# Storing the first eight finished row tiles one place earlier in the transfer order of a streamed matmul with scale and addend

## The chip, the cores and the metric

The kernel runs on one core of a Trainium2 chip. The metric is the device time of one execution in microseconds; a lower one is better. Three runs of the kernel before the change took 209.27, 209.72 and 210.06 us, a median of 209.72 us. A further execution was recorded by the profiler.

## The reference

```
batch, m, k, n = 16, 512, 1024, 768
x      : (16, 512, 1024) float32
weight : (1024, 768)     float32
add    : (16, 512, 768)  float32
out = scale * matmul(x, weight) + add_value      # scale = 0.1
```

With the batch flattened, 8192 rows of 1024 numbers are multiplied by a 1024 x 768 weight; the product is scaled and an addend of the same shape as the result is added.

## The kernel before

**Tiling.** The 8192 rows are 64 row tiles of 128 rows, numbered 0 to 63 (T, line 53). In three blocks (BLOCKS, line 9) a partition of the on-chip memory holds consecutive rows of the operand, so that a transfer of eight row tiles is one run of 32 KB for each partition for x, and of 24 KB for addends and results. In the text "rows 32 to 39" means row tiles 32 to 39 of x, "addends" those of add_value, "results" those of the output.

**Memory.** `xs` is a ring of 16 row tiles of x (X_SLOTS, line 10). `ao` is a ring of 32 row tiles (A_SLOTS, line 11), in which an addend is overwritten by its result: addends 32 to 39 go to the place of results 0 to 7 and can be loaded only after these are stored. `va` has two buffers of four row tiles in bfloat16, `xt` four transposed row tiles, `mm` four products in PSUM.

**Engines.** There is no scheduler: each engine has its own program, written out by hand, and all meet in semaphores.

- SyncE (`sync_engine`, line 120) issues every transfer in the order of the string STREAM (line 22), in which `x32+8` means rows 32 to 39, `a` addends, `w` the weight and `o` results. Ahead of each transfer it waits for whatever that transfer needs: for x, that ScalarE and GpSimd have moved away the rows whose slots are overwritten (lines 128 and 129); for addends from 32 on, that the results of the same slots have landed in memory (line 135); for results, that VectorE has made them (line 137). An engine's waits are in order, so everything behind a waiting transfer waits as well. All 28 transfers go to one hardware queue. Each transfer signals its landing on one of eight semaphores in turn ("lanes", line 83), and before a lane is used again SyncE waits for the earlier transfer on it (line 125).
- ScalarE and GpSimd (`mover`, line 140) cast x to bfloat16 and regroup it, each one half of a move of four row tiles (MOVE, line 20): move 8 takes rows 32 to 35, move 9 rows 36 to 39. A move waits for the landing of its rows (line 146) and for the `va` buffer (line 148), which comes free when the pairs of two moves ago have been transposed.
- VectorE (`vector_engine`, line 160) casts the weight, transposes two row tiles at a time (`turn`, line 169) and joins product and addend (`finish`, line 182). Pair p is row tiles 2p and 2p + 1; pair 16 holds rows 32 and 33. The order is finish(p), then turn(p + 2).
- TensorE (`tensor_engine`, line 219) multiplies pair after pair; pair p needs turn(p) and, for its place in PSUM, finish(p - 2).

The last transfer, results 60 to 63, is issued behind all of these (line 243).

Of the kernel before, what the change touches and what calls it, by code (L numbers as in the profile page):

```python
# [19 lines left out]
MOVE = 4  # L20

STREAM = """
    x0+4 w0+8 x4+8 a0+8 a8+8 x12+4 x16+8 a16+8 x24+8 a24+8 x32+8 o0+8 o8+8 a32+8 x40+8
    a40+8 x48+8 x56+4 o16+8 o24+8 a48+4 x60+4 a52+4 a56+8 o32+16 o48+4 o52+8 o60+4
"""

# [252 lines left out]
```

## Time and profile before

| | us |
|---|---|
| median of the three runs | 209.72 |
| lowest and highest run | 209.27 and 210.06 |
| profiled execution, its own time | 209.87 |
| its span in the profile | 208.1 |
| busy in that span: TensorE matmul | 167.7 (81%) |
| busy: VectorE | 122.9 (59%) |
| busy: ScalarE | 139.3 (67%) |
| busy: GpSimd | 139.9 (67%) |

The span runs from the first to the last thing that the profiler saw; 209.87 less 208.1 lies outside it. PE is TensorE, DVE VectorE, ACT ScalarE, POOL GpSimd; SPq is the queue of instructions of SyncE, which issues the transfers. Digits in strips are tenths of a slice, 40 slices to a span. The table of transfers gives for each group the number of issues, the kilobytes of one, and the median time from the issue to the landing, waiting in the queue included. A timeline row gives the start, the length, engine, line and operation, what is written and read, the number of instructions and, in brackets, the idle time ahead of the first and what ended it.

### The profile page before, as it was taken

What the parts mean: (1) busy time and instruction counts of PE and PEld (TensorE: products, weight loads), DVE (VectorE), ACT (ScalarE), POOL (GpSimd) and SP (SyncE); (2) the same over time, 40 slices, a digit from 0 to 9 for tenths busy, and PEclk for the clock granted to TensorE, in tenths of its full rate; (3) what the DMA queues carried; (4) which work ended last, traced back from release to release, by engine and by line L of the source; (5) the groups of instructions that cost most, each with busy time, mean ns of one, the idle gap of its engine ahead of it and who ended that gap; (6) DMA issues with size and microseconds to landing.
All of it is one profiled execution on the core that took longest, in us unless ns stands there. A gap on an engine that the chain in (4) does not pass through costs nothing.

```text
span 208.1 us, 2174 instructions
## 1 busy us (share of the span) xinstructions
PE 167.7 (81%) x1008; PEld 50.4 (24%) x512; DVE 122.9 (59%) x66; ACT 139.3 (67%) x153; POOL 139.9 (67%) x156
## 2 busy tenths in 40 slices
PE   0001994969999999999999999994999999999500
PEld 0000231313333333333333333321333333333100
DVE  0037309646777777777777777738677759776300
ACT  2495199989799896969694069999998969000000
POOL 0399399999799997969694059999999979000000
PEclk9999999999999999999999999999999999999975
DMA  6999999999999999999999999999999999998993
GB/s 249 452 408 447 409 453 444 409 457 403 436 461 409 425 463 416 367 411 439 439 427 438 419 441 450 403 428 447 435 409 432 427 439 449 449 453 364 454 411 161
DMA packets 4035, 87.06 MB, mean 418 GB/s; under 512 B 448, under 2 KB 448, under 8 KB 448
## 3 DMA queue, kind: packets, MB, share of 16 engines
q1 hardware_dynamic: 4032, 87.03, 97.9%
q14 instruction: 3, 0.02, 0.0%
HBM read 61.87 MB, written 25.17 MB: 418 GB/s over the span
## 4 chain that ended last, share of the span: by engine, by line
DMA 43%; PE 25%; POOL 21%; issue 3%; DVE 2%; SPq 1%; POOLq 0%; DVEq 0%
DMA xs<-in_x_dram 31%; POOL va L157 21%; PE mm L232 16%; DMA out_dram<-ao 12%; PE mm L207 9%; DVE xt L177 1%; DVE ao L188 1%; SPq L115 0%; SPq L113 0%; SPq L117 0%; POOLq L150 0%; SPq L106 0%; DVEq L106 0%; SPq L274 0%; SPq L237 0%
## 5 line engine op out<-in xcount | busy, mean ns | idle before, releaser
L232 PE MATMUL mm<-w_bf,xt 128*128 128x512 bf16 x496 | 163.8, 382 | 26.9 <-DVE w_bf L167 19.8
L157 POOL CAST va<-xs 32x1024 bf16<-32x1024 f32 (+1 forms) x152 | 139.7, 919 | 36.8 <-DMA xs<-in_x_dram 22.4
L157 ACT CAST va<-xs 32x1024 bf16<-32x1024 f32 (+1 forms) x152 | 138.0, 908 | 36.6 <-DMA xs<-in_x_dram 23.4
L207 PE MATMUL mm<-w_bf,xt 128*128 128x256 bf16 x512 | 140.2, 274 | 0.8
L232 PEld LDWEIGHTS mm<-w_bf,xt 128*128 128x128 bf16 x512 | 50.4, 98 | 144.6 <-issue 138.7
L177 DVE STREAM_TRANSPOSE xt<-va 128x1024 f32<-128x1024 f32 x32 | 65.2, 2038 | 32.0 <-POOL va L157 30.6
L188 DVE SCALAR_TENSOR_TENSOR ao<-mm,ao 128x1536 f32<-128x1536 f32 x32 | 56.0, 1754 | 42.5 <-PE mm L207 39.4
L167 DVE CAST w_bf<-ao 128x3072 bf16<-128x3072 f32 x2 | 3.8, 1948 | 0.0
L143 ACT ACT_TABLE_LOAD x1 | 1.3, 1283 | 0.9 <-SPq L237 0.9
L260 POOL MEMSET const-float32-0.0<- 128x1 f32 x1 | 0.1, 98 | 0.2 <-issue 0.2
L260 POOL MEMSET const-bfloat16-1.0<- 128x1 bf16 x1 | 0.1, 101 | 0.0
L260 POOL MEMSET const-float32-1.0<- 128x1 f32 x1 | 0.1, 98 | 0.0
L260 POOL MEMSET const-uint8-127<- 128x1 uint8 x1 | 0.1, 98 | 0.0
## 6 DMA issues: line engine op xcount, KB each, us to landing
xs<-in_x_dram SPq DMA_DIRECT2D x6, 4096.0 KB, 20.8
ao<-in_add_value_dram SPq DMA_DIRECT2D x7, 3072.0 KB, 25.2
out_dram<-ao SPq DMA_DIRECT2D x5, 3072.0 KB, 24.8
xs<-in_x_dram SPq DMA_DIRECT2D x4, 2048.0 KB, 13.3
out_dram<-ao SPq DMA_DIRECT2D x1, 6144.0 KB, 33.9
ao<-in_weight_dram SPq DMA_DIRECT2D x1, 3072.0 KB, 14.1
ao<-in_add_value_dram SPq DMA_DIRECT2D x2, 1536.0 KB, 14.6
out_dram<-ao SPq DMA_DIRECT2D x2, 1536.0 KB, 19.8
```

The costliest lines, as they stand in the source:

```text
L143: eng.preload_act_table(mybir.ActivationFunctionType.Copy)
L157: copy(va[q % VA_BUFS][32 * b:32 * b + 32, t:t + step, a, :], src[32 * a:32 * a + 32, t:t + step, b, :]).then_inc(count, step // 2)
L167: eng.tensor_copy(w_bf[:, h:h + 4, :], ao[:, W_SLOT + h:W_SLOT + h + 4, :]).then_inc(casts, 4)
L177: eng.transpose(xt[:, 2 * half:2 * half + 2, :, :].rearrange("p i c (a m) -> p i c a m", a=4), pairs.rearrange("p i a (k c) -> p i c a k", ...
L188: eng.scalar_tensor_tensor(a, mm[:, q:q + 2, 0:N], float(scale), a, op0=mybir.AluOpType.mult, op1=mybir.AluOpType.add).then_inc(made, 2)
L207: return eng.add_instruction(mybir.InstMatmult(name=nc.get_next_instruction_name(), engine=eng.engine, ins=[eng.lower_ap(weights), eng.low ...
L232: eng.matmul(mm[:, q, 0:CUT], piece, w_bf[:, j, 0:CUT], **flags)
L260: nc = _bacc.Bacc("TRN2", target_bir_lowering=False, num_devices=1)
```

## The change

One word of the transfer order changes its place. Results 0 to 7 (`o0+8`) are issued ahead of rows 32 to 39 (`x32+8`) instead of behind them; results 8 to 15 follow behind these rows. Number and sizes of the transfers, slots, waits of each kind and the programs of the other engines stay. Since lanes are dealt out in the order of the list, results 0 to 7 and rows 32 to 39 exchange theirs (lanes 2 and 3), and the waits on them follow.

```diff
 STREAM = """
-    x0+4 w0+8 x4+8 a0+8 a8+8 x12+4 x16+8 a16+8 x24+8 a24+8 x32+8 o0+8 o8+8 a32+8 x40+8
+    x0+4 w0+8 x4+8 a0+8 a8+8 x12+4 x16+8 a16+8 x24+8 a24+8 o0+8 x32+8 o8+8 a32+8 x40+8
     a40+8 x48+8 x56+4 o16+8 o24+8 a48+4 x60+4 a52+4 a56+8 o32+16 o48+4 o52+8 o60+4
 """
```

## The prediction

> **What bounds the kernel now.** I read the page first: the busy strip of the transfers and the table of queues.
>
> ```profile
> span 208.1 us, 2174 instructions
> ...
> DMA  6999999999999999999999999999999999998993
> ...
> q1 hardware_dynamic: 4032, 87.03, 97.9%
> ```
>
> The 16 transfer engines are busy for 97.9% of the span, in nine tenths or more of nearly every slice, all from one queue. PE, the next busiest, has 81%. So the bound to test is the stream of 87.03 MB: an order of transfers can save time only where this stream pauses or slows, and lose time only where it makes it pause. The second view is the timeline of SyncE around the change, which says when each transfer was issued.
>
> ```profile
> 53.63 0.33 SPq L115 DMA_DIRECT2D xs<-in_x_dram  x1
> 54.00 0.43 SPq L117 DMA_DIRECT2D ao<-in_add_value_dram  x1
> 72.09 0.33 SPq L115 DMA_DIRECT2D xs<-in_x_dram  x1
> 72.52 0.85 SPq L118 DMA_DIRECT2D out_dram<-ao  x2
> 97.37 0.34 SPq L117 DMA_DIRECT2D ao<-in_add_value_dram  x1
> 97.81 0.70 SPq L115 DMA_DIRECT2D xs<-in_x_dram  x1
> 104.65 0.33 SPq L117 DMA_DIRECT2D ao<-in_add_value_dram  x1
> 111.81 0.33 SPq L115 DMA_DIRECT2D xs<-in_x_dram  x1
> ```
>
> In the order of the list these are rows 24 to 31, addends 24 to 31, rows 32 to 39, results 0 to 7 and 8 to 15 (one row; the two issues are 0.47 us apart), addends 32 to 39, rows 40 to 47, addends 40 to 47, rows 48 to 55. The table of transfers, asked for one issue at a time, gives the time to landing of the first seven and the ninth, in this order:
>
> ```profile
> xs<-in_x_dram SPq DMA_DIRECT2D x1, 4096.0 KB, 18.3
> ao<-in_add_value_dram SPq DMA_DIRECT2D x1, 3072.0 KB, 25.2
> xs<-in_x_dram SPq DMA_DIRECT2D x1, 4096.0 KB, 17.9
> out_dram<-ao SPq DMA_DIRECT2D x1, 3072.0 KB, 24.8
> out_dram<-ao SPq DMA_DIRECT2D x1, 3072.0 KB, 31.6
> ao<-in_add_value_dram SPq DMA_DIRECT2D x1, 3072.0 KB, 14.5
> xs<-in_x_dram SPq DMA_DIRECT2D x1, 4096.0 KB, 23.8
> ...
> xs<-in_x_dram SPq DMA_DIRECT2D x1, 4096.0 KB, 26.8
> ```
>
> Issue plus time to landing gives 71.9, 79.2, 90.0, 97.3, 104.6, 111.9, 121.6 and, for rows 48 to 55, 138.6 us. The differences are the time of one transfer at the head of the queue: 7.3 us for addends 24 to 31, 10.8 for rows 32 to 39, 7.3 each for the two stores and addends 32 to 39, 9.7 for rows 40 to 47. They follow one another in the order of issue with no hole, and a store costs what an addend load of its size does. Each was in the queue before its turn: rows 32 to 39 by 79.2 - 72.1 = 7.1 us, addends 32 to 39 by 104.6 - 97.4 = 7.2 us. The stream does not run dry here.
>
> It does not at its end either; the last two issues are:
>
> ```profile
> 187.00 0.33 SPq L118 DMA_DIRECT2D out_dram<-ao  x1
> ...
> 197.66 0.33 SPq L118 DMA_DIRECT2D out_dram<-ao  x1
> ...
> out_dram<-ao SPq DMA_DIRECT2D x1, 3072.0 KB, 16.6
> ...
> out_dram<-ao SPq DMA_DIRECT2D x1, 1536.0 KB, 9.5
> ```
>
> Results 52 to 59 land at 203.6; the last store was issued 5.9 us before that and lands at 207.2. So all that the engines make is ready with some 6 us to spare.
>
> **The change, step by step.** First: can results 0 to 7 be issued at their new place, right behind addends 24 to 31 (issue 54.00 + 0.43)? Their lane was last used by rows 4 to 11, long landed; they need finish(3).
>
> ```profile
> 46.76 1.70 DVE L188 SCALAR_TENSOR_TENSOR ao<-mm,ao 128x1536 f32<-128x1536 f32 x1
> ...
> 67.96 1.76 DVE L188 SCALAR_TENSOR_TENSOR ao<-mm,ao 128x1536 f32<-128x1536 f32 x1 [1.47 <-PE mm L207]
> ```
>
> That ended at 48.5, so the store goes out at about 54.5 without a wait, and nothing behind it on SyncE is held up. Rows 32 to 39 then wait for moves 0 to 5 as before and go out at 72.1; results 8 to 15 follow at 72.5 (finish(7) ended at 69.7). The store's issue moves from 72.5 to 54.5, where SyncE only waited for GpSimd: 0 us on any path.
>
> Second: the queue. Addends 24 to 31 land at 79.2 as before. Then results 0 to 7 take 7.3 us, to 86.5; rows 32 to 39 take 9.7 (as rows 40 to 47) to 10.8 us (as here), to 96.2 or 97.3; results 8 to 15 to 103.5 or 104.6. Behind those the order and the bytes are the same. I take 97.3 and 104.6, since nothing says that the slow stretch of 10.8 goes away. Rows 32 to 39 are thus 7.3 us later, results 0 to 7 are 10.8 us earlier, and the sum over the three is unchanged: 0 us.
>
> Third: what is fed earlier. Addends 32 to 39 wait for the landing of results 0 to 7 and can go out at 86.6 instead of 97.4. Their turn in the queue comes at 104.6 both times, so their lead grows from 7.2 to 18 us, and nothing is gained, because the lead was not used up before. Rows 40 to 47 stood behind them on SyncE; they go out at 91.0, when move 7 is done (82.24 + 8.69 in the rows below), for a turn at 111.9. Also 0 us.
>
> Fourth: what is fed later. Moves 8 and 9 need rows 32 to 39.
>
> ```profile
> 82.24 8.69 POOL L157 CAST va<-xs 32x1024 bf16<-32x1024 f32 x8 [1.42 <-DVE xt L177]
> 92.63 8.69 POOL L157 CAST va<-xs 32x1024 bf16<-32x1024 f32 x8 [1.70 <-DVE xt L177]
> 103.03 8.70 POOL L157 CAST va<-xs 32x1024 bf16<-32x1024 f32 x8 [1.71 <-DVE xt L177]
> 121.75 3.27 POOL L157 CAST va<-xs 32x512 bf16<-32x512 f32 x5 [10.03 <-DMA xs<-in_x_dram]
> ```
>
> Before, move 8 began at 92.63, held by VectorE and not by the rows, which had been there for 2.6 us. After rows land GpSimd begins 0.2 us later (121.75 against 121.6). So move 8 now begins at 97.5, 4.9 us later, and ends at 106.2; move 9 ends at 114.9 instead of 111.7. Who waits for them:
>
> ```profile
> 104.36 1.76 DVE L188 SCALAR_TENSOR_TENSOR ao<-mm,ao 128x1536 f32<-128x1536 f32 x1 [1.50 <-PE mm L207]
> 106.04 2.04 DVE L177 STREAM_TRANSPOSE xt<-va 128x1024 f32<-128x1024 f32 x1
> 109.56 1.76 DVE L188 SCALAR_TENSOR_TENSOR ao<-mm,ao 128x1536 f32<-128x1536 f32 x1 [1.49 <-PE mm L207]
> ...
> 116.47 2.00 DVE L177 STREAM_TRANSPOSE xt<-va 128x1024 f32<-128x1024 f32 x1
> ```
>
> turn(16) at 106.04 needs move 8. It would begin at 106.3 at the latest, 0.3 us late, and end at 108.4; TensorE takes pair 16 up only when pair 15 is done, at 109.5 by the wait of finish(15). That leaves 1.1 us. turn(18) at 116.47 needs move 9, done at 114.9: 1.6 us left. Rows 48 to 55 wait on SyncE for move 9, so their issue goes from 111.8 to 115.0; their turn in the queue is 138.6 - 9.7 = 128.9. And from 121.75 the movers start afresh from rows 40 to 47, which land when they did: GpSimd's 10.03 us of waiting there shrink by 3.2, and the lateness ends.
>
> A rule of the Trainium skill speaks against this fourth step. The row is the landing of addends 32 to 39 behind a store, 7.3 us after it. The page DMA: Bandwidth & Descriptors, section "Queues, rings and completion order", says that a transfer's landing signal is written only after every earlier write of the same transfer engine, and its section on one DMA's anatomy gives about 2 us of fixed cost, mostly the receipt of the write, heaviest for HBM. By these, rows 32 to 39, now behind a store, could be reported up to 2 us later; as an estimate turn(16) would end at 110.4 and TensorE would wait 0.9 us. By the row there is no such delay, and the sum stays at 0.
>
> So the sum on the profiled execution is 209.87 + 0 = 209.87 us; it stands 0.15 above the median of the runs, and the prediction in terms of that median is 209.7.
>
> The zero of step four has a cover, with a price if it goes: TensorE loses what rows 32 to 39 come later than 97.3 + 1.1 = 98.4. Behind that lies another cover, TensorE's only wait in the second half:
>
> ```profile
> 143.33 0.39 PE L232 MATMUL mm<-w_bf,xt 128*128 128x512 bf16 x1 [2.68 <-DVE xt L177]
> ```
>
> It waits for rows from 40 on, not for those of the change, so up to 2.7 us of lateness vanish in it; the 5.9 us at the last store are the third.
>
> **Rivals.** *The hand-over from loads to stores costs.* The three stretches of the queue around the first store, in the view of engine time by windows:
>
> ```profile
> 79.30:90.00 10.70, 10.65 (x66) 3.21 (x33) 7.72 (x5) 8.86 (x10) 8.80 (x10) 1.00 0.95 379
> 90.00:97.30 7.30, 7.25 (x46) 2.25 (x23) 5.78 (x4) 5.29 (x6) 5.37 (x6) 1.00 1.01 434
> 97.30:104.60 7.30, 7.30 (x47) 2.15 (x22) 4.33 (x4) 5.34 (x6) 5.35 (x6) 1.00 1.02 438
> ...
> 86.00:88.00 2.00, 1.95 (x13) 0.59 (x6) 1.27 (x1) 1.95 (x3) 1.88 (x3) 1.00 0.94 279
> ```
>
> The last column is GB/s. Rows 32 to 39, the load just ahead of the first store, ran at 379 and took 10.8 - 9.7 = 1.1 us more than rows 40 to 47. If that is the price of turning from loads to stores, the change adds one such turn, at 79.2 behind addends 24 to 31: 209.7 + 1.1 = 210.8, slower, deciding if all 16 engines pay it at every turn. Against it: the dip to 279 lies at 86 to 88, before the load is through at 90.0, and the next such turn pays less:
>
> ```profile
> 132.46 0.33 SPq L115 DMA_DIRECT2D xs<-in_x_dram  x1
> ...
> xs<-in_x_dram SPq DMA_DIRECT2D x1, 2048.0 KB, 11.2
> ```
>
> Rows 56 to 59 land at 143.7, 5.1 us behind rows 48 to 55, where half of 9.7 is 4.85: 0.2 us. The turn costs between 0 and 1.1 us; I take 0, as the dip precedes the store, and keep 1.1 for the range.
>
> *The late rows stop the stream.* Rows 32 to 39 reach TensorE late, products and stores follow late. It decides only if they land after 98.4 + 2.7 + 5.9 = 107.0; at 108.5 it would give 209.7 + 1.5 = 211.2. For it speaks that they have lost their lead over move 8; against it, 107.0 is later than the end of results 8 to 15, which stand behind them.
>
> *The slow microsecond goes with the old order.* If the 1.1 us come from rows 32 to 39 standing just there, they may be lost in the new one: 209.7 - 1.1 = 208.6, faster. For it: it is the only dip of this size in the rows above. Against it: every turn from load to store remains, and a dip tied to a moment stays.
>
> *The change does not do what it says.* The store is issued early but the engines serve rows 32 to 39 beside it rather than behind it. Then the rows land between 90.0 and 97.3, and with the same bytes the time is again 209.7. Against it, landings follow the order of issue in every row above.
>
> **How the numbers follow.** The forecast, no change and 209.7, gets 0.72; the hand-over 0.11, the late rows 0.02, the lost dip 0.11, the rival without effect 0.04. Half a per cent, 1.05 us, is what a measurement of this kernel can tell from no change: three runs already spread over 0.8 us. A hand-over at its lower price of 0.2 us stays within it; I give that 0.03 of the 0.11. So faster is 0.11, slower 0.08 + 0.02 = 0.10, and the same 0.72 + 0.04 + 0.03 = 0.79. The one unknown cost, the dip, sets the range: 208.6 where it goes, 210.8 where it comes twice; outside are the late rows.
>
> **What would show it.** Right: results 0 to 7 issued at about 54.5 and landed at about 86.5; rows 32 to 39 landed at 96.2 to 97.3; addends 32 to 39 issued near 86.6, rows 40 to 47 near 91.0, and the latter landed near 121.6 as before; move 8 on GpSimd released by the rows and not by VectorE; TensorE without a new wait at 109.5; the queue busy for about 98%. Wrong: a landing of rows 40 to 47 that differs from 121.6 by more than 1 us, a hole in the strip of the transfers behind 79 us, TensorE waiting at pair 16, or a last store issued after results 52 to 59 have landed.

## The result, and the profile after

| | before | after |
|---|---|---|
| median of 21 runs each, us | 209.31 | 210.03 |
| lowest and highest | 209.09 and 210.06 | 209.19 and 210.49 |
| profiled execution, own time and span | 209.87 and 208.1 | 210.11 and 208.3 |

The ratio of the two times is 1.0026, with a 95% interval of 1.0017 to 1.0034: slower by 0.54 us (0.36 to 0.71), less than half a per cent, but outside what chance explains. It is not the quotient of the two medians, which differ by 0.72 us; here and below the argument goes by the ratio and its interval. The profiled execution of before is a further one and slower than all but one of the 21, so the two traces differ by only 0.2 us in span; the difference of the kernels is to be looked for in where the traces lose time, not in their ends.

The page of the kernel after, first line and table of queues:

```profile
span 208.3 us, 2174 instructions
...
q1 hardware_dynamic: 4032, 87.03, 97.9%
```

The queue is as full as before. The timeline of SyncE, start and length in us:

```profile
53.68 0.33 SPq L115 DMA_DIRECT2D xs<-in_x_dram  x1
54.05 0.43 SPq L117 DMA_DIRECT2D ao<-in_add_value_dram  x1
54.59 0.38 SPq L118 DMA_DIRECT2D out_dram<-ao  x1
72.14 0.33 SPq L115 DMA_DIRECT2D xs<-in_x_dram  x1
72.56 0.38 SPq L118 DMA_DIRECT2D out_dram<-ao  x1
87.81 0.33 SPq L117 DMA_DIRECT2D ao<-in_add_value_dram  x1
91.09 0.33 SPq L115 DMA_DIRECT2D xs<-in_x_dram  x1
```

These are rows 24 to 31, addends 24 to 31, results 0 to 7, rows 32 to 39, results 8 to 15, addends 32 to 39 and rows 40 to 47. The table of transfers, asked for one issue at a time, gives their time to landing in the same order:

```profile
xs<-in_x_dram SPq DMA_DIRECT2D x1, 4096.0 KB, 18.4
ao<-in_add_value_dram SPq DMA_DIRECT2D x1, 3072.0 KB, 26.3
out_dram<-ao SPq DMA_DIRECT2D x1, 3072.0 KB, 33.2
xs<-in_x_dram SPq DMA_DIRECT2D x1, 4096.0 KB, 26.0
out_dram<-ao SPq DMA_DIRECT2D x1, 3072.0 KB, 32.9
ao<-in_add_value_dram SPq DMA_DIRECT2D x1, 3072.0 KB, 24.9
xs<-in_x_dram SPq DMA_DIRECT2D x1, 4096.0 KB, 31.3
```

Issue plus time gives the landings 72.1, 80.4, 87.8, 98.1, 105.4, 112.7 and 122.4. Two loads took longer than their size asks for: addends 24 to 31 took 8.3 us instead of 7.3, rows 32 to 39 took 10.4 instead of 9.7. Each is the load just ahead of a store. Before the change there was one such load here, rows 32 to 39 with 10.8 us. The slow microsecond has moved with the first store, from 86 to 88 us to 77 to 79, and a second, smaller one has appeared at the second. The window of the kernel after, to be held against the 279 GB/s of 86 to 88 us before:

```profile
77.00:79.00 2.00, 2.00 (x14) 0.59 (x6) 0.57 (x1) 1.95 (x3) 1.88 (x3) 1.00 1.03 344
```

The signals of landing show whom it hits. A transfer is worked off by 16 engines, and each adds its signal when its share has landed (each trace holds 448 such signals for 28 transfers). The time from the first signal to the last, here called the lag, is how far the last engine is behind the first (worked out from the semaphore events of the two traces, us):

```
landing of            before   after
rows 24 to 31          1.04     1.12
addends 24 to 31       1.05     1.81   <- a store follows, after
results 0 to 7         1.62     1.63
rows 32 to 39          1.59     2.47   <- a store follows, both
results 8 to 15        1.28     2.25
rows 48 to 55          1.62     2.49
rows 56 to 59          1.79     2.47   <- a store follows, both
addends 56 to 63       2.25     2.50   <- a store follows, both
results 60 to 63       2.29     2.39
first signal of it   204.91   205.01
```

The first engine is done at 204.9 to 205.0 both times; the span ends when the last one is. The packets of the change's second turn from loads to stores show it at work: from 95.29 us the engines in front send their first packets of the store, and of the 17 packets of rows 32 to 39 that start between 93.96 and 95.37 twelve take the usual 1.21 us, while five take 1.37 to 1.97. At the first store of the run all 16 engines are slowed: the 16 packets of addends 24 to 31 that start between 76.93 and 77.39 take 1.06 to 2.07 us instead of 0.92.

GpSimd and VectorE around move 8 and pair 16, in the timeline of the kernel after:

```profile
98.33 17.45 POOL L157 CAST va<-xs 32x1024 bf16<-32x1024 f32 x16 [7.33 <-DMA xs<-in_x_dram]
...
104.43 1.76 DVE L188 SCALAR_TENSOR_TENSOR ao<-mm,ao 128x1536 f32<-128x1536 f32 x1 [1.49 <-PE mm L207]
107.16 2.08 DVE L177 STREAM_TRANSPOSE xt<-va 128x1024 f32<-128x1024 f32 x1 [0.97 <-POOL va L157]
109.63 1.76 DVE L188 SCALAR_TENSOR_TENSOR ao<-mm,ao 128x1536 f32<-128x1536 f32 x1 [0.40 <-PE mm L207]
```

Move 8 waits for the rows and turn(16) for move 8, but finish(15) comes at 109.63 instead of 109.56. The late rows did not stop TensorE there: it shows no wait between 100 and 120 us.

### The profile page after: what moved, and what is told of

The parts are those of the page before. It is cut to its first block, busy times and chain, and to the rows that moved or that the text cites. A ratio compares the mean times of both kernels' runs of the same rounds, so it can differ in the third digit from the quotient of the medians.

```text
span 208.3 us, 2174 instructions
## 1 busy us (share of the span) xinstructions
PE 170.3 (82%) x1008; PEld 50.7 (24%) x512; DVE 122.8 (59%) x66; ACT 139.3 (67%) x153; POOL 139.9 (67%) x156
## 3 DMA queue, kind: packets, MB, share of 16 engines
q1 hardware_dynamic: 4032, 87.03, 97.9%
## 4 chain that ended last, share of the span: by engine, by line
PE 41%; DMA 26%; POOL 21%; DVE 5%; issue 2%; SPq 0%; DVEq 0%; POOLq 0%
PE mm L232 26%; DMA xs<-in_x_dram 26%; POOL va L157 21%; PE mm L207 14%; DVE xt L177 3%; DVE ao L188 2%; SPq L113 0%; SPq L115 0%; DVEq L106 0%; POOLq L150 0%; SPq L274 0%; SPq L106 0%; SPq L237 0%
## 5 line engine op out<-in xcount | busy, mean ns | idle before, releaser
L232 PE MATMUL mm<-w_bf,xt 128*128 128x512 bf16 x496 | 166.2, 385 | 26.8 <-DVE w_bf L167 19.9
```

The lines of the kernel that those rows point to most:

```text
L232: eng.matmul(mm[:, q, 0:CUT], piece, w_bf[:, j, 0:CUT], **flags)
```

## The experiments

Every time beside a ratio is the median of its runs, and the ratio stands against the kernel before, run on the same chip. Theory 1 is the hand-over: each place where the list turns from a load to a store costs in the transfers. Such a place is called a turn from here on; it has nothing to do with VectorE's `turn`. The list of before has three turns, that of the change four. Theory 2 is the late rows, which cost through TensorE.

**Both stores early.** Three turns, rows 32 to 39 later still.

```diff
-    ... a24+8 x32+8 o0+8 o8+8 a32+8 ...
+    ... a24+8 o0+8 o8+8 x32+8 a32+8 ...
```

> Results 0 to 7 and 8 to 15 both go ahead of rows 32 to 39, so the list turns from loads to stores three times, as before the change, but rows 32 to 39 come 14.6 us later than before it, twice the change's 7.3. Theory 1, the hand-over (each place where a load is followed by a store costs about 0.5 us in the transfer engines): ratio 1.000, at most 1.001. Theory 2, the late rows (the lost half microsecond comes through TensorE, which gets rows 32 to 39 late): slower than the change's 1.0026, about 1.005.

210.71 us, 1.0047 (1.0029 to 1.0065). This is theory 2's number, but the trace shows that the turns did not make it: the lag at results 52 to 59 is 1.85 us, against 2.29 before and 2.51 with the change. What failed is the end; the last two issues and their times to landing in this execution, at 211.55 us the slowest of its eleven:

```profile
203.77 0.33 SPq L118 DMA_DIRECT2D out_dram<-ao  x1
...
out_dram<-ao SPq DMA_DIRECT2D x1, 3072.0 KB, 10.4
out_dram<-ao SPq DMA_DIRECT2D x1, 1536.0 KB, 5.1
```

Results 52 to 59, issued at 193.11, landed at 203.5, and the last store went out 0.3 us after that: the queue had run dry. So late rows can cost, and here they do; whether they do in the change, whose last store goes out in time, needs a kernel in which TensorE has time to spare.

**A turn elsewhere.** Four turns, rows 32 to 39 on time.

```diff
-    ... x48+8 x56+4 o16+8 o24+8 a48+4 ...
+    ... x48+8 o16+8 x56+4 o24+8 a48+4 ...
```

> The order of before around rows 32 to 39, but rows 56 to 59 put between results 16 to 23 and 24 to 31: four turns from loads to stores, as with the change, and rows 32 to 39 on time. Theory 1, the hand-over: ratio about 1.0026. Theory 2, the late rows: 1.000, since rows 56 to 59 land at about 151 and are needed at 158.

209.91 us, 1.0013 (1.0000 to 1.0026): half of theory 1's price, but the interval reaches from theory 2's 1.0000 to theory 1's 1.0026. It decides nothing by itself. In its trace the lag grows from 1.44 us at addends 40 to 47 to 1.78 at rows 48 to 55 and 2.53 at rows 56 to 59, the two loads that stand ahead of a store there.

**Five turns, and their control.**

```diff
-    ... x24+8 a24+8 x32+8 o0+8 o8+8 ...
+    ... x24+8 o0+4 a24+8 o4+4 x32+8 o8+8 ...      (five turns)
+    ... x24+8 a24+8 x32+8 o0+4 o4+4 o8+8 ...      (control)
```

> Results 0 to 3 go ahead of addends 24 to 31 and results 4 to 7 behind them, results 8 to 15 behind rows 32 to 39: five turns from loads to stores, and rows 32 to 39 exactly as late as with the change. Theory 1, the hand-over: about 1.005 (two more turns than before, 1.1 us). Theory 2, the late rows: the change's 1.0026.

> Control for the run with five turns: the order of before, with results 0 to 7 stored in two transfers of four, one behind the other; three turns. Both theories: 1.000. What is above it is the price of one more transfer and has to be taken off the run with five turns.

210.27 us, 1.0027 (1.0014 to 1.0040), and for the control 209.30 us, 1.0000 (0.9989 to 1.0012). The split costs nothing that can be seen. Theory 1 missed here, its 1.005 lies outside the interval: the turn beyond the change's, with the first two around stores of half the size, added nothing that can be seen.

**TensorE with half the work.** The order of before, of the change and of both stores early, with half the sum:

```diff
-                for j in range(KJ):
+                for j in range(0, KJ, 2):
...
-                    flags = dict(start=(j == 0), stop=(j == KJ - 1))
+                    flags = dict(start=(j == 0), stop=(j == KJ - 2))
```

> The order of before; TensorE multiplies only four of the eight parts of the sum over 1024, so the results are those of half the sum, and TensorE takes some 2.6 us for a pair instead of 5.2. All transfers are the same. It takes TensorE and its lateness away from the end of the stream. Both theories: 1.000, the base for the next two.

> The same half of the sum with the order of the change. Theory 1, the hand-over (the last transfer engines fall further behind at each place where a load is followed by a store): still about 0.5 us above half_before, ratio near 1.0026, since the transfers are the same. Theory 2, late rows reaching the end through TensorE: equal to half_before, since TensorE has more than 50 us to spare.

> The same half of the sum with both stores ahead of rows 32 to 39. In the full kernel this order gave 1.0047, and in its trace the queue ran dry ahead of the last store. Theory 1, the hand-over (three, as before): equal to half_before. Theory 2, late rows through TensorE: equal to half_before as well. Told apart from both: if the place of the first store or the lateness of rows costs something in the transfers themselves, it is above half_before.

Before's order: 209.54 us, 1.0004 (0.9992 to 1.0016). The change's: 209.97 us, 1.0028 (1.0017 to 1.0040). Both early: 209.16 us, 0.9992 (0.9981 to 1.0002). In the second the last two issues were these:

```profile
183.67 7.21 SPq L118 DMA_DIRECT2D out_dram<-ao  x2
...
out_dram<-ao SPq DMA_DIRECT2D x1, 3072.0 KB, 20.0
```

The one at 183.67 lands at 203.7, and the last store is issued near 190.5: all is ready 13 us early, and the change still costs what it cost, 1.0028 against the 1.0004 of its base, with intervals that do not overlap. With both stores early the rows are twice as late (15.2 us in place of 8.1, by their landings), the turns are three, and it costs nothing. This decides between the theories: the half microsecond of the change lies in the transfers and does not come through TensorE, and it is there with four turns and not with three. It is no fixed price of each turn, as the run with five turns shows.

**The change and the turn elsewhere.**

```diff
-    ... a24+8 x32+8 o0+8 ... x48+8 x56+4 o16+8 o24+8 ...
+    ... a24+8 o0+8 x32+8 ... x48+8 o16+8 x56+4 o24+8 ...
```

> The order of the change and, beside it, rows 56 to 59 between results 16 to 23 and 24 to 31: five turns from loads to stores, each with a full store of eight row tiles. Theory 1, the hand-over: the prices add up or nearly so, the change's 1.0026 and the 1.0013 of the run with the later split alone: 1.003 to 1.005. Theory 2: the change's 1.0026.

210.54 us, 1.0058 (1.0045 to 1.0071). Theory 2's 1.0026 lies outside the interval, so the direction is theory 1's. That it is more than the sum 1.0039 of the two alone says little, since their intervals together reach to 1.0060.

**Transfers alone.** Four kernels without computation, whose only program is that of SyncE: `a0` to `a24`, then eight loads of x and eight stores, in one of two orders. Two of them have one transfer more at the start.

```diff
+    a0+8 a8+8 a16+8 a24+8 x0+8 x8+8 x16+8 ... x56+8 o0+8 o8+8 ... o56+8     (grouped)
+    a0+8 a8+8 a16+8 a24+8 x0+8 o0+8 x8+8 o8+8 ... x56+8 o56+8               (alternating)
...
+        eng.dma_start(xs[0:2, 8:16, :], rows(x_v, 8, 8)[0:2])               (one engine behind)
```

> Transfers alone, no computation: four addend loads, then all eight loads of eight row tiles of x, then eight stores of eight; the results are copies of addends, and the weight is not loaded. 71.3 MB, one turn from load to store. Expected 71.3 of 87.0 MB of the stream, some 166 us for the bytes and about 170 us in all; it is the base for the next three. Both theories say nothing of it alone.

> The same transfers, loads of x and stores in turn: eight turns from load to store instead of one. Theory 1, the hand-over (an engine that is behind loses more at each such place): 7 turns by 0.2 to 0.7 us, 1.5 to 5 us above moves_grouped. Rival, that the cost of the change does not lie in the transfers: within 0.3 us of moves_grouped. If a turn costs only where an engine is already well behind: below 1.5 us, and more in moves_alternating_behind.

> As moves_grouped, with one more transfer at the start, of two partitions, 32 KB each, which puts at most two of the 16 transfer engines 1.2 us (or one of them 2.4) behind the others. With one turn the lag stays what it is: 1.2 to 2.5 us above moves_grouped, plus one turn's 0.2 to 0.7.

> As moves_alternating, with the same lag at the start. If the loss at a turn grows with the lag that is there, the difference to moves_grouped_behind is clearly larger than that of moves_alternating to moves_grouped. If a turn costs the same whatever the lag, the two differences are equal.

171.58 us grouped, 175.28 alternating: 3.70 us for seven more turns, 0.53 each on average, with the same bytes. This is inside theory 1's 1.5 to 5 us and far from its rival's 0.3. The queue rows of the two pages, grouped first, then alternating:

```profile
q1 hardware_dynamic: 2880, 71.30, 98.2%
```

```profile
q1 hardware_dynamic: 2880, 71.30, 96.9%
```

The lag at the end is 0.62 us grouped and 3.54 alternating; the first engine's last signal comes at 168.4 and 169.2. So of the longer time 2.9 us is lag, and 0.8 is lost by all engines. The turns do not share it evenly: the lag rose from 0.62 to 2.22 us at the third turn and from 2.11 to 2.99 at the fourth, and hardly at the next three.

With engines put behind at the start: 173.88 grouped, 2.30 above grouped without and as expected, and 175.72 alternating, 1.84 us more or 0.26 a turn. Neither of the two outcomes named for this pair came, a larger difference or the same; it is half as large. That a turn costs more where an engine is behind would fit the single turn (grouped, the lag grew there from 1.92 to 2.69, against 0.41 to 0.66 without, in one execution each), but not many: both alternating kernels end near the same lag, 3.54 and 3.80. The lag seems to fill up, which would also fit the five turns; that it is the reason was not tried.

## Why the prediction was wrong

**First step, the issue of the store: right.** 54.59 against 54.5, nothing held up behind it.

**Second step, the queue: wrong, and here it failed.** That "the sum over the three is unchanged: 0 us" treats the queue as one stream with one rate. It is 16 streams, and the time is that of the slowest. The premise was set at the start, where an order can "lose time only where it makes it pause": the queue stayed at 97.9%, never paused, and lost 0.54 us. The step behind it is in the first rival: "The turn costs between 0 and 1.1 us; I take 0, as the dip precedes the store". Both the zero and its reason are refuted. The dip is tied to the first store though it begins ahead of it: with the store 10 us earlier it came at 77 to 79, again before the load was through. And a turn has a price: 0.53 us on average in transfers alone, 0.54 (0.36 to 0.71) for the one that the change adds. The 0.2 us read from rows 56 to 59 was no zero either.

The profiled executions tie the time to the lag. Time of the execution, its lag at the last landing, and the difference:

```
                       us      lag   less the lag
half the sum, before  208.78   1.27   207.51
control               209.13   1.48   207.65
half, both early      209.22   1.73   207.49
before                209.87   2.29   207.58
half, the change      209.98   2.47   207.51
the change            210.11   2.39   207.72
turn elsewhere        210.25   2.64   207.61
change and turn       210.33   2.81   207.52
five turns            210.64   3.02   207.62
```

Nine executions of nine orders or programs differ by 1.9 us, and without the lag by 0.23. (Both stores early in the full kernel is not among them: its queue ran dry.) These are single executions, some at the edge of their kernel's runs: the first is the fastest of its twelve, the last the slowest. They show where the time of an execution lies; that a turn more costs time is shown by the runs.

The landings also show where the lag is made. In the ten traces with computation the loads ahead of a store, together, took longer than the usual 9.7, 7.3 and 4.9 us of loads of 4096, 3072 and 2048 KB by 0.1 to 1.6 us with three turns (five traces), by 1.7 to 1.8 with four (three) and by 2.0 to 2.1 with five (two). A single turn took anything from nothing to 1.0 us. The loads just behind a store and not ahead of another kept the usual time of their size within 0.2 us in all ten.

**Third step, what is fed earlier: right.** Addends 32 to 39 went out at 87.8 and rows 40 to 47 at 91.1, and neither gained anything.

**Fourth step, what is fed later: right at pair 16, too small behind it.** Rows 32 to 39 landed at 98.1, inside the 98.4 that was allowed. The delay of up to 2 us that the prediction weighed for a load behind a store does not show: their first signal came 9.6 us after that of results 0 to 7, no more than the 9.7 that such a load takes. The section of the Trainium skill's page DMA: Bandwidth & Descriptors on one DMA's anatomy gives the 2 us for transfers that GpSimd issues, and these are issued by SyncE. But rows 40 to 47 landed 0.9 us later by the lag (122.4 against 121.6), and TensorE's wait at 143 us, the second cover, grew where it should have shrunk. TensorE's waiting row, and the windows behind it (the columns as in the prediction, the granted clock third from last), after the change:

```profile
144.20 0.61 PE L232 MATMUL mm<-w_bf,xt 128*128 128x512 bf16 x1 [3.33 <-DVE xt L177]
...
144.00:148.00 4.00, 3.80 (x14) 0.98 (x8) 3.69 (x3) 3.90 (x5) 3.76 (x5) 0.57 1.06 455
```

and before:

```profile
144.00:148.00 4.00, 4.00 (x27) 1.17 (x12) 2.87 (x2) 3.90 (x5) 3.76 (x5) 1.00 1.01 436
```

After 3.33 us of waiting instead of 2.68 the granted clock fell to 0.57 for these 4 us, 14 matmuls instead of 27 were counted, and TensorE came out 2.5 us late (the last store 200.12 against 197.66). The third cover held it:

```profile
200.12 0.33 SPq L118 DMA_DIRECT2D out_dram<-ao  x1
...
out_dram<-ao SPq DMA_DIRECT2D x1, 3072.0 KB, 14.3
```

Results 52 to 59, issued at 189.46, landed at 203.8, 3.65 us behind the last issue; 5.9 had been there.

**The rivals.** The hand-over was the right mechanism, at a half of its upper price, and got 0.11. The late rows did not decide here; with both stores early they did, with rows landing at 104.6 and not only after 107.0. There TensorE waited 6.1 us at pair 16, and the granted clock fell behind it, which was not in that sum:

```profile
116.00:120.00 4.00, 4.00 (x14) 1.00 (x7) 3.13 (x2) 3.90 (x5) 3.82 (x4) 0.50 1.06 457
```

The lost dip fell: it came along with the store. That the change does what it says is shown by the landings. The forecast of no change within half a per cent held, as did the range; that there is no loss at all did not. None of the signs of being wrong came either: rows 40 to 47 landed 0.9 us late where more than 1 was asked, the strip had no hole, TensorE did not wait at pair 16, and the last store was issued in time. They watched for a queue that pauses, with margins wider than the price; the landing of addends 24 to 31, 80.4 in place of 79.2, was the first to differ by more than a few tenths.

## What to carry to other kernels

Where one queue is full from end to end, count the places at which its order turns from loads to stores, and keep stores together as far as their slots allow: here one more group of stores cost about half a microsecond, on average and not each time. Read a transfer's landings engine by engine, since a full queue ends with its slowest engine and a busy share of 98% hides two microseconds of lag. A dip that comes shortly ahead of an event may still belong to it; moving the event is the way to tell.

## What was not expected of the hardware

At a turn, loads are slowed while other engines already store: packets of 32 KB took up to 1.97 us instead of 1.21. At the first store of a run the slow packets begin ahead of the first store packet in the records, by 1.3 us after the change (76.9 against 78.2) and by 3.0 before it (85.0 against 88.1), and they meet all 16 engines; why is open. No run separates the turn back from stores to loads, since a list has one of these fewer than turns; but the loads there kept their time, as said above, so the traces show no price for it.

Two fetches of instructions, 8 KB each, at 58.9 and 59.2 us in the trace of before, shared transfer engines with data: two packets that start as they end, at 59.17 and 59.59, took 1.33 and 1.28 us instead of 0.91, and the lag rose from 0.53 to 1.05 us and stayed.

TensorE's clock fell after the wait of 3.33 us but not after that of 2.68. The Trainium skill, page TensorE: Matmul & The Clock Gate, section "Part 1: The HAM clock gate", says that an idle window of about 3.4 us brings the clock down to half; the two rows agree with that roughly. But in the kernel with the turn elsewhere a wait of 2.25 us, shorter than the 2.68, was followed by a granted clock of 0.59 between 144 and 148 us, so the length of one wait does not decide it.
